# Rotating 96 images by 90 degrees: loads moved from the SyncE queue to the GpSimd queue, the last slab first

## The chip, the cores and the metric

The kernel runs on one core of a Trainium2 chip. A core has compute engines (TensorE or PE, VectorE or DVE, ScalarE or ACT, GpSimd or POOL) and a queue engine, SyncE or SP, that only issues transfers and waits. Transfers between the chip's main memory (HBM) and the on-chip memory (SBUF, 128 partitions) are carried out by 16 DMA engines, whoever issues them. The metric is the device time of one execution in microseconds (us); lower is better. The times given for the kernel before are 123.1, 123.25 and 123.28 us: a median of 123.25 us.

## The reference

```python
def setup_inputs():
    batch, c, h, w = 32, 3, 256, 256
    return {"x": np.random.randn(batch, c, h, w).astype(np.float32)}

def reference(x):
    return np.rot90(x, k=-1, axes=(-2, -1)).astype(np.float32)
```

There are 32 x 3 = 96 images of 256 x 256 float32 values. Each is turned clockwise by a quarter: the output's row c is the input's column c read from the bottom row upwards. Nothing is computed; 25.17 MB are read, rearranged and 25.17 MB are written.

## The kernel before, in words

**Slabs.** The 96 images are cut into 12 slabs, 0 to 11, of 8 images or 2 MB each (`n_slabs` = 12, `last` = 11). A slab lies in SBUF as one buffer of 128 partitions x 4096 values, and is called `units[n]`. Two layouts are in use. In the short one a partition holds pieces of 8 image rows (8 KB in one run), and in the long one a transfer of 1 MB fills every second partition with 16 image rows (16 KB in one run). Slabs 0, 1 and 2 are loaded short and stored long; the others are loaded long. All 12 slabs stay resident, so no load has to wait for a buffer.

**Loads.** All loads are issued by SyncE, in the order 0, 1, 2, 3, 7, 4, 5, 6, 8, 9, 10, 11 (line 86). Slabs 1 and 2 are one transfer of 2 MB each (line 88); every other slab is two transfers of 1 MB, one for each `i` (lines 92 and 96). The first transfer of slab 11 is cut once more, into 14/16 and 2/16 of its bytes, and the first of these two is remembered as `mark`. The framework gives SyncE's transfers eight completion semaphores in turn, so a ninth transfer waits until the first has landed, and so on.

**Turning.** VectorE turns a slab with transposes of 32 x 32 blocks (line 118), two instructions for a slab or four for a pair of slabs; each handles 128 x 2048 values. The rest of the turn lies in the access patterns. The result of slab n goes to `home[n]`, which is the buffer of slab n-1 (already used up); that of slab 0 goes to PSUM (`turned0`). Slabs 8 and 9 are turned as a pair into the buffers of slabs 3 and 7, and slabs 10 and 11 as a pair into the buffers of slabs 8 and 9. So the pair 8/9 can't be turned before slab 4's result, which stands in the buffer of slab 3, is stored.

**Stores.** All stores are issued by SyncE too, behind the loads in its queue, in the order 4, 3, 5, 6, 7, 1, 2, 8, 9, 10, 11, 0: 17 transfers of 1 or 2 MB (lines 124, 127, 130 and 132). The store of slab 4 waits for `mark`, so that stores begin when nearly all loads have landed (line 139). The result of slab 0 is copied by ScalarE from PSUM into the buffer of slab 11 (line 146) once VectorE has read that buffer, and it is stored last.

**Order on the queues.** SyncE works through its instructions in program order: an instruction that waits holds up all that follow. GpSimd does nothing in this kernel apart from four small fills of constants that the framework puts at its start.

Of the kernel before, what the change touches and what calls it, by code (L numbers as in the profile page):

```python
# [1 line left out]

# [4 lines left out]

@with_exitstack
def kernel(
    ctx: ExitStack,
    tc: tile.TileContext,
    x: bass.AP,
    out: bass.AP,
):

    nc = tc.nc
    fp32 = mybir.dt.float32

    B, C, H, W = x.shape
    P = nc.NUM_PARTITIONS
    RL, RS = 16, 8  # L50
    I = 2
    Q = P * RS // H
    n_slabs = B * C // (Q * I)
    last = n_slabs - 1
    F = RS * W
    long_st = (0, 1, 2)
    both = (8, 10)
    paired = [n + a for n in both for a in range(2)]

    rows_in = x.rearrange("b c h w -> (b c h) w")  # L60
    rows_out = out.rearrange("b c h w -> (b c h) w")

    def short(rows):
        return rows.rearrange("(n i p r) w -> n p i (r w)", i=I, p=P, r=RS)

    def long(rows):
        return rows.rearrange("(n i m r) w -> n i m (r w)", i=I, m=P // I, r=RL)

    ld_short, ld_long, st_short, st_long = short(rows_in), long(rows_in), short(rows_out), long(rows_out)

    units = [None] * n_slabs
    adjacent = [(3, 7), (8, 9), (10, 11)]
    pairs = []
    for us in adjacent + [(u,) for u in range(n_slabs) if all(u not in us for us in adjacent)]:
        pool = ctx.enter_context(tc.tile_pool(name=f"unit{us[0]}", bufs=1))
        held = pool.tile([P, len(us), I * F], fp32, name=f"u{us[0]}")
        for j, u in enumerate(us):
            units[u] = held[:, j]
        pairs.append(held)
    psum = ctx.enter_context(tc.tile_pool(name="psum", bufs=1, space=bass.MemoryType.PSUM))  # L80
    turned0 = psum.tile([P, I * F], fp32, name="turned0")

    def fours(t):
        return t.rearrange("p (i f) -> p i f", i=I)

    for n in (0, 1, 2, 3, 7, 4, 5, 6, *range(8, n_slabs)):
        if n in (1, 2):
            nc.sync.dma_start(out=fours(units[n]), in_=ld_short[n])
            continue
        for i in range(I):  # L90
            if n in long_st:
                ld = nc.sync.dma_start(out=fours(units[n])[:, i], in_=ld_short[n][:, i])  # L92
            else:
                cuts = (0, 14 * W, RL * W) if (n, i) == (last, 0) else (0, RL * W)
                for f0, f1 in zip(cuts, cuts[1:]):
                    ld = nc.sync.dma_start(out=units[n][i::I, f0:f1], in_=ld_long[n, i][:, f0:f1])
                    if f1 == 14 * W:
                        mark = ld

    home = [turned0] + units[:last]  # L100

    def turn(n):
        if n in long_st:
            src = fours(units[n]).rearrange("p i (r g c) -> p c r g i", r=RS, c=RL)
            dst = home[n].rearrange("p (c k r) -> p c r k", c=RL, r=RS)[:, :, ::-1, ::-1]
            parts, step = 2, RL // 2
        elif n in paired:
            if n not in both:
                return
            src = pairs[both.index(n) + 1].rearrange("p a (r g c) -> p c r g a", r=RL, c=RL)  # L110
            dst = pairs[both.index(n)].rearrange("p i (c k r) -> p c r k i", c=RL, r=RL)[:, :, ::-1, ::-1, :]
            parts, step = 4, RL // 4
        else:
            src = units[n].rearrange("p (r g c) -> p c r g", r=RL, c=RS)
            dst = fours(home[n]).rearrange("p i (c k r) -> p c r k i", c=RS, r=RL)[:, :, ::-1, ::-1, :]
            parts, step = 2, RS // 2
        for h in range(parts):
            nc.vector.transpose(out=dst[:, h * step : (h + 1) * step], in_=src[:, h * step : (h + 1) * step])  # L118

    def store(n):  # L120
        if n in paired:
            first = n if n in both else n - 1
            if n == first:
                nc.sync.dma_start(out=st_long[n].transpose([1, 0, 2]), in_=pairs[both.index(n)][::I])
                return
            for i in range(I):
                nc.sync.dma_start(out=st_long[n, i], in_=pairs[both.index(first)][n - first :: I, i])
        elif n in long_st:
            for i in range(I):
                nc.sync.dma_start(out=st_long[n, i], in_=home[n][i::I])  # L130
        else:
            return nc.sync.dma_start(out=st_short[n], in_=fours(home[n]))

    for n in range(both[0]):
        turn(n)
    for n in (4, 3, 5, 6, 7, 1, 2):
        st = store(n)
        if n == 4:
            tc.add_manual_dep(st.ins, mark.ins.name, mybir.DependencyInfo(
                mybir.DependencyClass.Sync, mybir.DependencyReason.SCHED_ONLY), reason="stores after loads")  # L140
    for n in range(both[0], n_slabs):
        turn(n)
        store(n)

    for i in range(I):
        nc.scalar.copy(out=fours(units[last])[:, i], in_=fours(turned0)[:, i])  # L146
    home[0] = units[last]
    store(0)


# [1 line left out]
_INS = ['x']  # L152
_OUTS = [((32, 3, 256, 256), 'float32')]


# [23 lines left out]
```

## Time and profile before

| | value |
|---|---|
| times of three runs | 123.1, 123.25, 123.28 us |
| profiled execution: span from first to last instruction | 121.4 us |
| difference of median and span | 1.8 us |
| bytes moved, DMA queue 1 (issued by SyncE) | 50.33 MB in 4800 packets, 98.0% of 16 engines' span |
| VectorE busy | 90.5 us (75%), 24 instructions |
| ScalarE busy | 4.9 us |
| GpSimd busy | 0.2 us |

The profile is of one execution. A packet is the unit in which a DMA engine's work is recorded: here one contiguous run of 8 or 16 KB (14 and 2 KB for the cut transfer), or the 4 bytes by which an engine reports that its share of a transfer is done. "SPq" is SyncE's instruction queue and "DVEq" VectorE's. A group of instructions is given as line, engine, operation and the names of what is written and read; "L118" is line 118. The table of windows cuts the span into stretches and gives for each the engines' busy time, the mean busy share of the 16 DMA engines (a little over 1 where packets overlap) and the bytes moved per time. A DMA transfer "lands" when its completion semaphore has its full count.

### The profile page before, as it was taken

Reading aid. Unit: us, or ns where it says so; the run is one execution under the profiler, and the core shown is the slowest. Engines: PE = TensorE matmul, PEld = TensorE weight load, DVE = VectorE, ACT = ScalarE, POOL = GpSimd, SP = SyncE. Lnnn points to the kernel's source line nnn. Section 1 sums busy time; section 2 is a strip of 40 time slices with the busy share of each in tenths; the row PEclk is TensorE's granted clock in tenths of the full one; section 3 lists DMA queues with packets and bytes.
Section 4 is the critical chain, followed back from the end, with each engine's and each line's share of the span. In section 5 each row is a group of like instructions: output and inputs, shape, how many; then the busy total and the mean of one; then the engine's idle time right before and its main releaser. Section 6 shows DMA issues by size and latency. Waiting matters only on the chain.

```text
span 121.4 us, 134 instructions
## 1 busy us (share of the span) xinstructions
DVE 90.5 (75%) x24; ACT 4.9 (4%) x3; POOL 0.2 (0%) x4
## 2 busy tenths in 40 slices
DVE  0029999999999999999999999999999960000000
ACT  0000000000000000000040000000000038000000
POOL 0000000000000000000000000000000000000000
DMA  3999999999999999999999999999999999999994
GB/s 84 416 432 424 426 459 432 432 432 426 426 432 426 416 421 432 421 426 450 403 424 426 426 429 429 421 432 424 464 426 432 432 432 432 432 432 432 432 432 178
DMA packets 4800, 50.33 MB, mean 414 GB/s; under 512 B 640, under 2 KB 640, under 8 KB 704
## 3 DMA queue, kind: packets, MB, share of 16 engines
q1 hardware_dynamic: 4800, 50.33, 98.0%
HBM read 25.17 MB, written 25.17 MB: 414 GB/s over the span
## 4 chain that ended last, share of the span: by engine, by line
DVE 55%; issue 17%; DMA 6%; DVEq 3%; ACT 2%; ACTq 1%; SPq 0%
DVE u L118 50%; DVE turned L118 6%; DMA u<-in_x_dram 6%; DVEq L174 3%; ACT u L146 2%; ACTq L174 1%; SPq L92 0%; DVEq L118 0%
## 5 line engine op out<-in xcount | busy, mean ns | idle before, releaser
L118 DVE STREAM_TRANSPOSE u<-u 128x2048 f32<-128x2048 f32 x22 | 83.4, 3861 | 0.3
L118 DVE STREAM_TRANSPOSE turned<-u 128x2048 f32<-128x2048 f32 x2 | 7.1, 3584 | 8.3 <-DMA u<-in_x_dram 8.3
L146 ACT COPY u<-turned 128x2048 f32<-128x2048 f32 x2 | 3.6, 1869 | 35.6 <-DVE u L118 35.6
L146 ACT ACT_TABLE_LOAD x1 | 1.3, 1283 | 62.3 <-DMA u<-in_x_dram 62.3
L163 POOL MEMSET const-uint8-127<- 128x1 uint8 x1 | 0.1, 103 | 0.0
L163 POOL MEMSET const-bfloat16-1.0<- 128x1 bf16 x1 | 0.1, 101 | 0.0
L163 POOL MEMSET const-float32-0.0<- 128x1 f32 x1 | 0.1, 99 | 0.2 <-issue 0.2
L163 POOL MEMSET const-float32-1.0<- 128x1 f32 x1 | 0.1, 99 | 0.0
## 6 DMA issues: line engine op xcount, KB each, us to landing
u<-in_x_dram SPq DMA_DIRECT2D x19, 1024.0 KB, 19.6
out_dram<-u SPq DMA_DIRECT2D x7, 2048.0 KB, 16.3
out_dram<-u SPq DMA_DIRECT2D x10, 1024.0 KB, 18.3
u<-in_x_dram SPq DMA_DIRECT2D x2, 2048.0 KB, 13.7
u<-in_x_dram SPq DMA_DIRECT2D x1, 896.0 KB, 19.3
u<-in_x_dram SPq DMA_DIRECT2D x1, 128.0 KB, 17.2
```

Source lines behind the costliest of these rows:

```text
L118: nc.vector.transpose(out=dst[:, h * step : (h + 1) * step], in_=src[:, h * step : (h + 1) * step])
L146: nc.scalar.copy(out=fours(units[last])[:, i], in_=fours(turned0)[:, i])
L163: nc = _bacc.Bacc("TRN2", target_bir_lowering=False, num_devices=1)
L174: with _tile.TileContext(nc) as tc:
```

## The change

The order of the loads becomes 11, 0, 1, 2, 3, 7, 4, 5, 6, 8, 9, 10. The two transfers of slab 11 are issued by SyncE. All others, 22 transfers of 1 MB, are issued by GpSimd, in the order given, with the option that the share of each DMA engine in a transfer is one packet (`single_packet=True`). Slabs 1 and 2 are loaded as two transfers each, and slab 11's first transfer is no longer cut. `mark` is now the first transfer of slab 10, the last but one that GpSimd issues. The stores stay on SyncE in their old order, which is now spelled out by ordering hints between one store and the next; the first waits for `mark`. VectorE's and ScalarE's work is the same.

```diff
-    for n in (0, 1, 2, 3, 7, 4, 5, 6, *range(8, n_slabs)):
-        if n in (1, 2):
-            nc.sync.dma_start(out=fours(units[n]), in_=ld_short[n])
-            continue
+    def pull(out, in_):
+        if in_slab == last:
+            return nc.sync.dma_start(out=out, in_=in_)
+        ld = nc.gpsimd.dma_start(out=out, in_=in_, single_packet=True)
+        if behind:
+            tc.add_manual_dep(ld.ins, behind[-1].ins.name, mybir.DependencyInfo(
+                mybir.DependencyClass.NoSync, mybir.DependencyReason.SCHED_ONLY), reason="order of the loads")
+        behind.append(ld)
+
+    behind = []
+    for in_slab in (last, 0, 1, 2, 3, 7, 4, 5, 6, *range(8, last)):
+        n = in_slab
         for i in range(I):
             if n in long_st:
-                ld = nc.sync.dma_start(out=fours(units[n])[:, i], in_=ld_short[n][:, i])
+                pull(out=fours(units[n])[:, i], in_=ld_short[n][:, i])
             else:
-                cuts = (0, 14 * W, RL * W) if (n, i) == (last, 0) else (0, RL * W)
-                for f0, f1 in zip(cuts, cuts[1:]):
-                    ld = nc.sync.dma_start(out=units[n][i::I, f0:f1], in_=ld_long[n, i][:, f0:f1])
-                    if f1 == 14 * W:
-                        mark = ld
+                pull(out=units[n][i::I], in_=ld_long[n, i])
+    mark = behind[-2]
...
+    tail = [mark]
+
+    def put(out, in_):
+        st = nc.sync.dma_start(out=out, in_=in_)
+        tc.add_manual_dep(st.ins, tail[0].ins.name, mybir.DependencyInfo(
+            mybir.DependencyClass.Sync if tail[0] is mark else mybir.DependencyClass.NoSync,
+            mybir.DependencyReason.SCHED_ONLY), reason="order of the stores")
+        tail[0] = st
...
     for n in (4, 3, 5, 6, 7, 1, 2):
-        st = store(n)
-        if n == 4:
-            tc.add_manual_dep(st.ins, mark.ins.name, mybir.DependencyInfo(
-                mybir.DependencyClass.Sync, mybir.DependencyReason.SCHED_ONLY), reason="stores after loads")
+        store(n)
```

In `store`, each `nc.sync.dma_start` becomes `put` with the same operands.

## The prediction

> **What bounds the kernel now.** I read the page first, from its top.
>
> ```profile
> span 121.4 us, 134 instructions
> DVE 90.5 (75%) x24; ACT 4.9 (4%) x3; POOL 0.2 (0%) x4
> DMA  3999999999999999999999999999999999999994
> q1 hardware_dynamic: 4800, 50.33, 98.0%
> ```
>
> VectorE is busy for three quarters of the span, the DMA engines in every slice but the first and the last. The chain of waits puts 55% on VectorE, but that chain ends in stores, and what holds them is the row of DMA. So I read the bytes per time by stage, in a table of windows (columns: stretch, its length, DVE, ACT and POOL busy, clock, DMA share, GB/s).
>
> ```profile
> 2.00:3.00 1.00, 0.00 (x0) 0.00 (x0) 0.00 (x0) 1.00 0.44 164
> 3.00:16.00 13.00, 7.71 (x3) 0.00 (x0) 0.00 (x0) 1.00 1.01 425
> 19.00:57.00 38.00, 37.83 (x11) 0.00 (x0) 0.00 (x0) 1.00 1.01 428
> 62.50:78.00 15.50, 15.47 (x5) 1.05 (x1) 0.00 (x0) 1.00 1.01 427
> 108.00:119.00 11.00, 0.00 (x0) 0.00 (x0) 0.00 (x0) 1.00 1.00 429
> ```
>
> Loads of 8 KB packets run at 425 GB/s and of 16 KB at 428; stores of 8 KB at 427 and of 16 KB at 429. There is no hole from 3 to 119 us, the turn from loads to stores included. The time is therefore a start, 50.33 MB at this rate, and an end; a change counts only if it alters the rate or opens a hole. For holes I read SyncE's waits and the timeline.
>
> ```profile
> SPq L96 <- DMA u<-in_x_dram: 32.5, 14, 4.5
> SPq L174 <- DMA out_dram<-u: 15.0, 5, 5.5
> SPq L132 <- DMA u<-in_x_dram: 13.9, 1, 13.9
> ```
>
> ```profile
> 0.73 0.88 SPq L92 DMA_DIRECT2D u<-in_x_dram  x2
> 8.25 7.08 DVE L118 STREAM_TRANSPOSE turned<-u 128x2048 f32<-128x2048 f32 x2 [8.25 <-DMA u<-in_x_dram]
> 15.36 83.70 DVE L118 STREAM_TRANSPOSE u<-u 128x2048 f32<-128x2048 f32 x22
> 59.46 11.13 SPq L132 DMA_DIRECT2D out_dram<-u  x5
> 99.10 0.63 SPq L124 DMA_DIRECT2D out_dram<-u  x1
> 102.76 2.67 SPq L130 DMA_DIRECT2D out_dram<-u  x2
> ```
>
> Fourteen loads wait for an earlier landing, and the first store waits 13.9 us for `mark`; neither empties the DMA engines. VectorE, once started, never stops until 99.1 us. The last store is issued some 16 us ahead of the end. In the packet records the first data starts at 1.77 us and the last ends at 120.3.
>
> **The sum's base.** The profiled span is 121.43 us, the median 123.25. The 1.82 us between them lie outside the profile, and I leave them as they are.
>
> **Part 1: rate of the 22 moved loads.** One engine's share of 1 MB is 64 KB: 8 packets in slabs 0 to 2, 4 in the others. At 425 GB/s an engine needs 8192 / (425/16) = 308.4 ns for 8 KB; at 428, 612.5 ns for 16 KB. Two small packets take 4.3 ns more than a large one, so a packet costs about 4.3 ns beside its bytes (3 to 6 with the rounding of the rates). With one packet for 64 KB, six transfers save 7 x 4.3 ns and sixteen save 3 x 4.3 ns: 0.18 + 0.21 = 0.39 us. All of it is on the path, since the DMA engines have no other idle time. No row shows a load issued by GpSimd, so this is bounded. Best: the 23.07 MB, which take 6.29/0.425 + 16.78/0.428 = 54.0 us, run at the best rate that the packet costs allow for stores (429 without 4.3 ns in 611 ns is 432 GB/s), 53.4 us, and 22 completion packets of 9 ns vanish as well: 0.8 us saved. Worst: the nearest row of a queue that is not fed by SyncE is the instruction queue, whose six 8 KB packets took 475 ns against 309 in the load queue. If each transfer lost these 166 ns once, uncovered, it would be +3.7 us. I take the saving of 0.39: the instruction packets ran one at a time before the span on an idle memory, while here up to eight transfers stand in line, and the first packets of SyncE's own loads (0.7 to 1.3 us) show that a cold packet says little about the stream.
>
> The Trainium skill ("DMA: Bandwidth & Descriptors", section "Why small descriptors are slow (HBM only)") gives about 3 cycles of overhead a packet and calls joining descriptors worthwhile only at 256 B or less; by its fabric clock of 850 MHz that is an estimated 3.5 ns, near the row's 4.3, and the sum would be 0.32 us. The same page ("Latency and other measured facts") speaks against the change: engines 7 and 15 are usually slower under GpSimd's descriptor rings; it gives no figure, and no row here can show it.
>
> **Part 2: the start.** SyncE issues slab 11 at the same 0.73 us, two issues as now, so data starts at the same 1.77 us. Its 2.1 MB keep the engines busy for 4.9 us, to 6.7. GpSimd's fills end at 0.43; its issue is not shown. The nearest rows are SyncE's, from 0.47 (load) to 1.4 us (store in pieces), and from issue to first data SyncE takes 1.04, so GpSimd's first data should come by 2.9 us. It costs nothing up to 6.7, and the excess one for one after that. The ramp could differ by 0.3 us either way (six of sixteen engines started 0.7 us late; slab 11 has half as many packets). Taken: 0.
>
> **Part 3: VectorE starts later.** Slab 0 now shares the engines with slab 11: between +0 and +4.9 us, if all of slab 11 goes first. What covers it is the queue of stores. After VectorE ends (99.1) the stores of slabs 10, 11 and 0 follow, 6.3 MB or 14.7 us; data ends near 120.0, so the engines run dry at 105.3 and the store must be issued by 104.2. That is 5.1 us of cover for at most 4.9. Slab 0's store needs the copies and issues behind it (3.6 + 1.3 + 1.0 = 5.9 us), covered by 9.8 us of slabs 10 and 11. Pair 8/9 needs slab 4 stored, which landed at 67.1 against 70.5. Price 0; past 5.1 us it is one for one. Later slabs come every 4.9 us and are used every 7.6, so they are never late.
>
> **Part 4: queues.** GpSimd issues 22 loads, of which 14 wait for the eighth before them, as 14 do on SyncE now. With seven or eight 1 MB transfers in line (17 us) an issue may take up to 2.44 us, the time of 1 MB, before it limits anything. Nothing else stands in that queue. SyncE's 17 stores stand behind the wait for `mark`, as they stood behind the loads.
>
> **Part 5: loads to stores.** `mark` landed at 59.39, 0.47 us behind its last data; the store was issued at 59.46, and its first packet ran at 61.26, when the loads ran out. With 1.04 us from issue to data it was ready at 60.5, some 0.76 us early. Now 1 MB follows `mark` in place of 1.125 MB: 0.3 us less, 0.45 early. Cost 0, unless a GpSimd landing reports over 0.45 us later than a SyncE one.
>
> **Part 6: the end.** SyncE waits for every completion semaphore; there are up to eight more, in pairs of 0.065 us (event at 120.64, next at 120.70). Between 0, if they stand ahead of the last store's, and 0.26. I take one, 0.06: the early ones are paired with late ones today.
>
> **Sum.** -0.39 + 0.06 = -0.33 us: a span of 121.1 and a time of 122.92 us, 0.27% less.
>
> **Rivals.**
>
> *The ring-fed queue is slower (other side).* Place: the 54 us of the moved loads. If each transfer, or one of the 16 engines, loses more than it saves, the loads stretch and everything behind them moves. It decides from (0.33 + 0.25) / 22 = 26 ns a transfer, a load rate under about 425 GB/s. At half the 166 ns it is +1.8 us less the saving: 124.7; in full 126.6. For it: the 475 ns row. Against: eight transfers in line. Where it decides I put it at 124.2, a mild loss of 60 ns a transfer (+1.3 us) less the rest.
>
> *The option or queue changes no rate.* The DMA share is already 1.01 and packets overlap, so the 4.3 ns may belong to runs of bytes rather than to packets. Then parts 2 to 6 alone are left: 123.3.
>
> *GpSimd and VectorE stand in each other's way.* Transposes run back to back (3861 ns each, 0.3 us idle in all). If GpSimd could prepare a transfer only between two of them, one transfer in 3.9 us would replace one in 2.44: 14 x 1.4 = +20 us, about 143. No row shows GpSimd working beside a transpose.
>
> The Trainium skill ("SBUF — State Buffer", section "SBUF: two separate sides") warns of just this for VectorE's two-port modes; a transpose at 2048 values in 3.86 us is 0.53 a ns, under one per cycle of the 0.96 GHz that it states, so by the rule it should not bite: 0 instead of 20 us.
>
> *A hole at the turn or the start.* A landing 0.45 + x late, or first GpSimd data at 6.7 + x, costs x: 123.5 to 124.5.
>
> **How the numbers follow.** Less than 0.2%, about 0.25 us, cannot be told from no change. Forecast with its mechanism: 0.48, of which 0.40 falls beyond 0.2% (its own range 122.2 to 123.1). No rate change: 0.12. Slower queue: 0.28. Engines in each other's way: 0.04. Hole: 0.08. Faster: 0.40 and 0.02 from luck at the start, 0.42. Same: 0.08 and 0.10: 0.18. Slower: 0.40. The low end, 122.2, is 123.25 less 0.8 and the 0.3 of the ramp; the high end takes in the slower queue up to half of its upper bound and a bit, 125.2. Outside stay the far part of the slower queue (0.10), the collision (0.04) and a little below.
>
> **What would show it.** Right: load stretches at 430 GB/s or more, loads over by 60.5 to 61 us, no dip in the first five slices or at the turn, VectorE starting between 9 and 13 us and ending by 104, fewer packets. Wrong: a load stretch under 425 GB/s, a slice under 9 before the stores, waits of VectorE on loads after its start, or longer transposes. The forecast falls if engines drift apart in the loads, which the mean rate hides but the turn would show.

## The result

The changed kernel takes 123.96 us (median of 4 runs, 123.83 to 124.05) against 123.2 us before (123.1 to 123.28): the ratio is 1.0062 with a 95% interval of 1.0048 to 1.0077. It is slower by 0.76 us, or 0.6%. The forecast was 122.92, faster.

### The profile page after: what moved, and what is told of

The parts are those of the page before. It is cut to its first block, busy times and chain, and to the rows that moved or that the text cites. A ratio compares the mean times of both kernels' runs of the same rounds, so it can differ in the third digit from the quotient of the medians.

```text
span 122.2 us, 145 instructions
## 1 busy us (share of the span) xinstructions
DVE 90.5 (74%) x24; ACT 4.9 (4%) x3; POOL 11.9 (10%) x26
## 3 DMA queue, kind: packets, MB, share of 16 engines
q0 software_dynamic: 2144, 23.07, 44.5%
## 4 chain that ended last, share of the span: by engine, by line
DVE 41%; DMA 25%; issue 15%; DVEq 3%; ACT 2%; ACTq 1%; POOL 1%; PEldq 0%
DVE u L123 41%; DMA u<-in_x_dram 25%; DVEq L185 3%; ACT u L157 2%; ACTq L185 1%; POOL u L89 1%; DVEq L123 0%; PEldq L185 0%
## 5 line engine op out<-in xcount | busy, mean ns | idle before, releaser
L123 DVE STREAM_TRANSPOSE turned<-u 128x2048 f32<-128x2048 f32 x2 | 7.1, 3586 | 13.4 <-DMA u<-in_x_dram 13.4
L89 POOL DMA_DIRECT2D u<-in_x_dram x22 | 11.7, 534 | 31.5 <-DMA u<-in_x_dram 30.7
## 6 DMA issues: line engine op xcount, KB each, us to landing
out_dram<-u SPq DMA_DIRECT2D x10, 1024.0 KB, 13.5
```

Source lines behind the costliest of these rows:

```text
L89: ld = nc.gpsimd.dma_start(out=out, in_=in_, single_packet=True)
```

## The profile after

The page of the changed kernel, its lines on busy time, slices, DMA queues and VectorE's first work:

```profile
span 122.2 us, 145 instructions
DVE 90.5 (74%) x24; ACT 4.9 (4%) x3; POOL 11.9 (10%) x26
DMA  3999999999999999999999999999999999999993
...
q1 hardware_dynamic: 2608, 27.26, 53.0%
q0 software_dynamic: 2144, 23.07, 44.5%
...
L123 DVE STREAM_TRANSPOSE turned<-u 128x2048 f32<-128x2048 f32 x2 | 7.1, 3586 | 13.4 <-DMA u<-in_x_dram 13.4
```

The span grew from 121.4 to 122.2 us. The row of DMA still has no slice under 9 between the first and the last. GpSimd's 23.07 MB are a queue of their own (q0). Its 2144 packets are 768 of 8 KB, 1024 of 16 KB and 352 completions: one data packet for each run of bytes. Nothing was merged into packets of 64 KB.

The table of windows of the changed kernel (stretch, length, busy times, clock, DMA share, GB/s):

```profile
3.00:16.00 13.00, 2.59 (x1) 1.28 (x1) 3.59 (x7) 1.00 0.98 413
19.00:57.00 38.00, 37.83 (x11) 0.00 (x0) 5.35 (x11) 1.00 1.01 431
62.50:78.00 15.50, 15.43 (x5) 0.00 (x0) 0.00 (x0) 1.00 1.01 429
108.00:119.00 11.00, 0.00 (x0) 0.00 (x0) 0.00 (x0) 1.00 1.01 429
```

This view books whole packets, so a few GB/s either way mean nothing. If each packet record is spread over its own time, the loads from 24 to 57 us run at 428.4 GB/s in both kernels, and a load packet takes the same median time from GpSimd's queue after as from SyncE's before, 613 ns for 16 KB and 309 ns for 8 KB. The first line, 413 against 425 before, holds the later start: spread in the same way, the loads from 4 to 16 us run at 425.8 GB/s against 426.2. The stream is as fast as it was, and no faster.

The timeline of the changed kernel:

```profile
0.73 1.20 SPq L88 DMA_DIRECT2D u<-in_x_dram  x2
1.23 4.31 POOL L89 DMA_DIRECT2D u<-in_x_dram  x8 [0.79 <-PEq L185]
...
13.41 7.08 DVE L123 STREAM_TRANSPOSE turned<-u 128x2048 f32<-128x2048 f32 x2 [13.41 <-DMA u<-in_x_dram]
...
20.52 83.67 DVE L123 STREAM_TRANSPOSE u<-u 128x2048 f32<-128x2048 f32 x22
...
60.01 49.76 SPq L128 DMA_DIRECT2D out_dram<-u  x17
104.22 3.63 ACT L157 COPY u<-turned 128x2048 f32<-128x2048 f32 x2 [92.62 <-DVE u L123]
```

SyncE's first two loads took 1.20 us to issue; the two it issued first before took 0.88. VectorE starts at 13.4 in place of 8.25 and ends at 104.2 in place of 99.1.

So where are the 0.76 us? The packet records and landings of the two profiled executions cut each span into three parts:

```
                          before    after    difference
first data                  1.77     2.10      +0.33
first to last data        118.50   118.54      +0.04
last data to last landing   0.35     0.35       0.00
last landing to end         0.81     1.19      +0.38
span                      121.43   122.18      +0.75
```

The 118.5 us in which data move are as long as before, to 0.04 us. The start and the end became longer.

What SyncE does in the end can be seen in the instructions of the framework's closing line (minimum/median/maximum ns, first and last start). Before:

```profile
L174 SPq EVENT_SEMAPHORE  x7: 17/28/28, 110.9 to 121.4; - x7
L174 POOLq EVENT_SEMAPHORE_RANGE_CLEAR  x1: 93/93/93, 121.1 to 121.1; - x1
```

After:

```profile
L185 SPq EVENT_SEMAPHORE  x11: 17/28/28, 109.8 to 122.1; - x11
L185 POOLq EVENT_SEMAPHORE_RANGE_CLEAR  x1: 136/136/136, 121.8 to 121.8; - x1
```

There are four more waits, and clearing takes 43 ns more. What counts is their order. Each instruction waits for two semaphores; the times are their starts, after the last data:

```
before: last landing 120.62 on semaphore 107
  120.637 waits for 107 and 102;  120.702 the drain that follows
after: last landing 120.99 on semaphore 110
  121.005 waits for 110 and 103
  121.066 111, 102;  121.126 112, 101;  121.187 113, 100
  121.246 114, 99;   121.308 116, 109;  121.373 the drain that follows
```

All of the later five pairs had been satisfied long before, the latest DMA landing among them at 113.7 us. They still cost 0.061 us each, one after the other, because they stand behind the last store's semaphore.

## The experiments

My theory after the result was: the start costs 0.33 us because SyncE's first load now has the long form (every second partition, 16 KB each); the end costs 0.38; the option and GpSimd's queue cost and gain nothing. The rivals were that GpSimd's queue, or the option, slows the loads in itself, and that only the order matters. For the time of each comparison the kernel before ran beside it, at 123.24 to 123.29 us.

**Without the option.**

```diff
-        ld = nc.gpsimd.dma_start(out=out, in_=in_, single_packet=True)
+        ld = nc.gpsimd.dma_start(out=out, in_=in_)
```

> The changed kernel without the single-packet option on GpSimd's loads. Theory (start + end): the option does nothing that can be seen, since the changed kernel's own records show 8 and 16 KB packets and between 6 and 9 us the two queues share at 2:1, the ratio of one 16 KB piece to one 8 KB piece; so 123.9 to 124.0 us, first data at 2.1, the same 2:1 sharing, loads at 428 GB/s. Rival (the option costs or saves time): loads differ from 428 by more than 2 GB/s, the sharing changes, and the time moves by over 0.3 us.

Measured: 124.01 us, ratio 1.006 (1.0047 to 1.0073), first data at 2.10 us, 428.4 GB/s. Its page:

```profile
DMA packets 4752, 50.33 MB, mean 412 GB/s; under 512 B 656, under 2 KB 656, under 8 KB 656
...
q0 software_dynamic: 2144, 23.07, 44.5%
```

The number of packets is the same as with the option. From 6 to 9 us, where both queues have work, the packet records give these rates (SyncE's packets are 16 KB in the first two kernels and 8 KB in the third, GpSimd's are 8 KB):

```
GB/s, 6 to 9 us                GpSimd   SyncE
changed kernel                   134      296
without the option               149      282
SyncE loads slab 0 (next run)    214      215
```

The engines alternate run by run, 1 to 2 where the runs are 8 and 16 KB and 1 to 1 where they are equal. That agrees with the Trainium skill ("DMA: Bandwidth & Descriptors", section "Queues, rings and completion order"), which has each engine change between queues after each packet, if a packet here is one run; the 9 to 17 descriptors a packet that the section calls typical don't fit these shares, where a descriptor is one run. Had GpSimd's packet been 64 KB beside SyncE's single runs of 16 KB, it would have been 4 to 1 for GpSimd. In this kernel the option does nothing that a record or a time shows.

**Slab 0 in place of slab 11 as SyncE's load.**

```diff
-        if in_slab == last:
+        if in_slab == 0:
-    for in_slab in (last, 0, 1, 2, 3, 7, 4, 5, 6, *range(8, last)):
+    for in_slab in (0, 1, 2, 3, 7, 4, 5, 6, *range(8, n_slabs)):
```

> The changed kernel with slab 0 in place of slab 11 as the one that SyncE loads first; slab 11 goes last on GpSimd's queue. Theory (start + end): first data returns to 1.77 us and VectorE starts near 8.3, while the end keeps its 1.54 us behind the last data: 123.5 to 123.65 us, a ratio to the kernel before of 1.003. Rival (GpSimd's queue itself slows the loads): 123.9 or more, as in the changed kernel. Rival (only slab 11 going first costs): 123.2.

Measured: 123.68 us, ratio 1.0034 (1.0022 to 1.0046). First data at 1.78 us, last landing to end 1.18. VectorE started only at 10.7, since GpSimd's slabs share the engines with slab 0's second half. The start is back and the end is not. The stretch of data was 0.19 us longer than in the kernel before: from 88 to 118 us the stores ran at 428.3 GB/s, against 430.9 before and 430.4 in the changed kernel, and no run shows why. The timeline:

```profile
0.74 0.87 SPq L88 DMA_DIRECT2D u<-in_x_dram  x2
1.24 4.31 POOL L89 DMA_DIRECT2D u<-in_x_dram  x8 [0.79 <-PEq L185]
```

**The order of the loads alone, GpSimd unused.**

```diff
-    for n in (0, 1, 2, 3, 7, 4, 5, 6, *range(8, n_slabs)):
+    for n in (last, 0, 1, 2, 3, 7, 4, 5, 6, *range(8, last)):
...
-                cuts = (0, 14 * W, RL * W) if (n, i) == (last, 0) else (0, RL * W)
-                for f0, f1 in zip(cuts, cuts[1:]):
-                    ld = nc.sync.dma_start(out=units[n][i::I, f0:f1], in_=ld_long[n, i][:, f0:f1])
-                    if f1 == 14 * W:
-                        mark = ld
+                ld = nc.sync.dma_start(out=units[n][i::I], in_=ld_long[n, i])
+                if (n, i) == (last - 1, 0):
+                    mark = ld
```

> The kernel before with its order of loads alone changed: slab 11 first and in two uncut transfers, the mark on slab 10's first transfer, all loads still issued by SyncE. Theory (start + end): first data at 2.1 us, the end as before (1.16 us): 123.45 to 123.65 us, with VectorE starting near 13.1 and no hole in the stores. Rival (GpSimd's queue is the whole cause): 123.2.

Measured: 123.68 us, ratio 1.0036 (1.0024 to 1.0048), with first data at 2.09 us:

```profile
0.72 1.21 SPq L94 DMA_DIRECT2D u<-in_x_dram  x2
1.98 1.25 SPq L92 DMA_DIRECT2D u<-in_x_dram  x2
```

The slow first issue belongs to the load of slab 11 and not to GpSimd, which issues nothing here. As the first on SyncE's queue, an issue of slab 11 takes 0.57 to 0.58 us and its first data come 0.79 us after, in every kernel that begins with it; one of slab 0 takes 0.39 to 0.41, and data come 0.64 after. Whether it's the larger runs, the stepping over every second partition or the place of slab 11 in memory was not tested apart, since no other long load went first. Nor does the form alone set the length of an issue: behind slab 11, the two of slab 0 took 0.59 and 0.62 us here. VectorE started at 13.5 and ended at 104.4, and the row of DMA has no hole. The end was 0.88 and not 0.81: 39 transfers in place of 40 left one pair behind the last landing. I had expected no change there, and this was the hint for what follows.

**Eight small transfers on GpSimd, added to the kernel before.** They add semaphores only, and nobody reads what they load.

```diff
+    few = ctx.enter_context(tc.tile_pool(name="few", bufs=1))
+    for k in range(8):
+        bit = few.tile([1, 64], fp32, name=f"bit{k}")
+        nc.gpsimd.dma_start(out=bit, in_=rows_in[k : k + 1, :64])
```

> The kernel before plus eight transfers of 256 bytes issued by GpSimd at the start, which nobody uses: they add eight completion semaphores and next to no data. Theory (start + end): SyncE waits at the end for five more pairs of semaphores, 0.061 us each, and their clearing takes 0.04 more: the end behind the last data grows from 1.16 to 1.5 us, the time to 123.5 to 123.7 us. Rival (the end is longer because 23 MB went through GpSimd's queue): the end stays at 1.16 us and the time at 123.2 to 123.3.

Measured: 123.87 us, ratio 1.0047 (1.0034 to 1.0061), and the expectation was wrong in its mechanism. There are as many waits as in the changed kernel:

```profile
L178 SPq EVENT_SEMAPHORE  x11: 17/28/28, 105.7 to 121.9; - x11
```

But the last landing was at 121.11 and the end 0.88 us later, so only 0.07 was added. The time went elsewhere: the stretch of data grew to 119.0 us. It had 413 GB/s between 5 and 10 us, where the small packets run, against 425 before (0.14 us), 428.1 from 88 to 118 us against 430.9 (0.2 us), and one engine ending 0.17 us after the rest. Why the late stores ran slower is not shown. The number of semaphores alone doesn't set the end. The place of the last store's semaphore does: here 115 was the last of SyncE's eight, as 107 is before. SyncE uses eight in turn; 40 transfers end on the eighth, 19 on the third.

**All loads on GpSimd.**

```diff
-        if in_slab == last:
-            return nc.sync.dma_start(out=out, in_=in_)
-    for in_slab in (last, 0, 1, 2, 3, 7, 4, 5, 6, *range(8, last)):
+    for in_slab in (0, 1, 2, 3, 7, 4, 5, 6, *range(8, n_slabs)):
```

> The changed kernel with all 24 loads on GpSimd, in the old order, nothing loaded by SyncE. In the changed kernel GpSimd's first packet ran at 5.2 us, 3.9 us after its first issue began at 1.23. Reading A (GpSimd's first transfer takes that long by itself): first data near 5.2 us, so 3.4 us later than before, and with a longer end about 127 us. Reading B (it was only held behind SyncE's packets, which were in the engines first): first data between 2.3 and 3.0 us, about 124.3 to 124.9 us. In both the loads run at 428 GB/s, and the end is about 1.6 us, since the last of 17 SyncE transfers uses the first of its eight semaphores.

Measured: 124.79 us, ratio 1.0129 (1.0106 to 1.0152). Reading B: first data at 2.63 us, 1.40 after the first issue began, with the end at 1.32 us behind the last landing (17 transfers end on the first of the eight semaphores). So GpSimd's first packets, which ran only at 5.0 to 5.4 us in each kernel that has SyncE loads in front, had been held back. Each time SyncE's first 1 MB was about through. Why the engines did not alternate before that isn't settled; they were busy meanwhile, so it cost nothing.

**Slabs 11 and 10 first.** This moves VectorE's start further.

```diff
-        if in_slab == last:
+        if in_slab in (last, last - 1):
-    for in_slab in (last, 0, 1, 2, 3, 7, 4, 5, 6, *range(8, last)):
+    for in_slab in (last, last - 1, 0, 1, 2, 3, 7, 4, 5, 6, 8, 9):
```

> The changed kernel with slabs 11 and 10 both loaded first by SyncE. This tests the cover of VectorE's late start, which the prediction put at an end of VectorE's work by 104.2 us. Theory: slab 0 is complete near 17.5 us, VectorE ends near 108.3, the DMA engines stand empty for 3 to 4 us before the store of slab 10, and the time is 127 to 128 us. Rival (late starts of VectorE are covered further than that): 124 us.

Measured: 128.63 us, ratio 1.0436 (1.0422 to 1.045), somewhat above the expected 127 to 128, since slab 0 was complete at 18.4 and not 17.5. Timeline and windows:

```profile
18.38 7.08 DVE L123 STREAM_TRANSPOSE turned<-u 128x2048 f32<-128x2048 f32 x2 [18.38 <-DMA u<-in_x_dram]
25.49 83.68 DVE L123 STREAM_TRANSPOSE u<-u 128x2048 f32<-128x2048 f32 x22
109.20 3.63 ACT L157 COPY u<-turned 128x2048 f32<-128x2048 f32 x2 [97.55 <-DVE u L123]
```

```profile
100.00:106.00 6.00, 6.00 (x3) 0.00 (x0) 0.00 (x0) 1.00 0.93 393
106.00:110.40 4.40, 3.17 (x1) 1.20 (x1) 0.00 (x0) 1.00 0.00 0
110.40:120.00 9.60, 0.00 (x0) 2.43 (x2) 0.00 (x0) 1.00 1.03 437
```

All 16 engines stand empty from 106.09 to 110.48 us, 4.39 us, until the store of slab 10 starts. VectorE ended 4.98 us later than in the changed kernel, so that kernel had 4.98 - 4.39 = 0.59 us of cover left.

**The changed kernel with 24 transfers on SyncE.**

```diff
-            put(out=st_short[n], in_=fours(home[n]))
+            for i in range(I):
+                put(out=st_short[n][:, i], in_=fours(home[n])[:, i])
```

> The changed kernel with the stores of slabs 3 to 7 cut into two transfers of 1 MB each, so that SyncE issues 24 transfers and not 19. SyncE's eight semaphores are used in turn and waited for at the end in the order of their numbers, so with 24 the last store has the last of them. Theory (the end is set by where the last store's semaphore stands): no pair is left to wait for after the last landing, the end behind the last data falls from 1.54 to 1.2 to 1.25 us and the time from 123.96 to 123.6 to 123.7. Rival (the mere number of semaphores sets it): end and time as in the changed kernel, 1.54 and 123.95.

Measured: 123.79 us, ratio 1.0042 (1.0029 to 1.0054). The semaphores are as many as in the changed kernel, and the part after the last landing fell from 1.19 to 0.88 us, as the theory has it. Four kernels differ here in the number of SyncE's transfers, beside eight semaphores of GpSimd, and their ends line up: 0.88 us with 24, the last on the eighth semaphore of SyncE; 1.06 with 21, on the fifth (two slabs first); 1.19 with 19, on the third; 1.32 with 17, on the first. That is 0.06 us a place. The time fell by 0.17 us, or by 0.25 if each kernel is taken against the kernel before that ran beside it. That is less than 0.31: in the profiled execution, the slowest of five, the stretch of data was 0.23 us longer, one engine ending 0.12 us after the others. Whether the cut stores do that, or it varies from run to run, this run alone can't tell; in the last but one run below the same cut stores had 118.47.

**The kernel before with 43 transfers.**

```diff
+            if n in (5, 6, 7):
+                for i in range(I):
+                    nc.sync.dma_start(out=st_short[n][:, i], in_=fours(home[n])[:, i])
+                return
```

> The kernel before with the stores of slabs 5, 6 and 7 cut into two transfers of 1 MB each: 43 transfers on SyncE in place of 40, nothing on GpSimd. Theory (where the last store's semaphore stands): it now has the third of eight, five pairs or so are waited for behind it, the end grows from 1.16 to about 1.45 us and the time from 123.2 to about 123.5. Rival (GpSimd's queue or its semaphores are needed for a longer end): 1.16 us and 123.2.

Measured: 123.39 us, ratio 1.0008 (0.9997 to 1.0019): too close to 1 to call it slower. Three pairs and not five came behind the last landing. With SyncE's eight semaphores alone, the third is waited for together with the fifth, and SyncE stood at that pair until the landing, with three pairs left; so the number of semaphores matters too, through the pairing. The end was 0.98 us in place of 0.81. The direction is as expected, the size is smaller, and only the profile shows it.

**Both terms undone, GpSimd's queue kept.** The edits of the second run and of the one with 24 transfers together.

> The changed kernel with both edits together: SyncE loads slab 0 first, and the stores of slabs 3 to 7 are cut in two, so that SyncE issues 24 transfers. 23.07 MB still go through GpSimd's queue. Theory (start + end, and no cost of GpSimd's queue): first data at 1.77 us, 1.22 us behind the last data, 123.3 to 123.5 us, within 0.2% of the kernel before. Rival (GpSimd's queue costs something of its own, which the two terms hid): 123.6 us or more, from a longer stretch of data or a load rate under 427 GB/s.

Measured: 123.37 us, ratio 1.0008 (0.9999 to 1.0017). Its page and windows:

```profile
span 121.6 us, 150 instructions
...
DMA  3999999999999999999999999999999999999994
```

```profile
19.00:57.00 38.00, 37.83 (x11) 0.00 (x0) 5.24 (x10) 1.00 1.01 429
```

First data at 1.77 us, 118.47 us of data, an end of 0.89 us behind the last landing; that landing came 0.47 us behind the last data, where the kernel before has 0.35, so that the two together are 1.36 and not the expected 1.22. This closes the account to within about 0.1 us: with start and end put right, 23.07 MB through GpSimd's queue cost no more than the measurement can tell, and gain nothing.

**Two issuers for slab 0**, on the kernel before, in search of a better start.

```diff
-                ld = nc.sync.dma_start(out=fours(units[n])[:, i], in_=ld_short[n][:, i])
+                ld = (nc.scalar if i else nc.sync).dma_start(out=fours(units[n])[:, i], in_=ld_short[n][:, i])
```

> The kernel before with the second transfer of slab 0 issued by ScalarE at the same time as SyncE issues the first. In the kernel before eight to ten engines take their first packet at 1.8 us and the others only at 2.5 to 2.7. If the late ones wait for more work to be issued, they start near 1.9 us, and the time falls by 0.1 to 0.3 us to 122.9 to 123.1. If not (they wait for memory, or share one unit that hands out work), the start is as before and the time 123.2 to 123.3.

Measured: 123.42 us, ratio 1.0018 (1.001 to 1.0027). ScalarE issued at the same 0.72 us as SyncE, but its packets began at 2.74 against 1.74, and the start didn't improve: from 3 to 4 us 343 GB/s were moved against 420 before, a loss of 0.18 us. In the profiled execution, the slowest of eleven, the stretch of data was 119.02 us. No version here beats the kernel before.

## Why the prediction was wrong

**Part 1, the saving of 0.39 us by larger packets: 0.** This is the first failed step. Without it the forecast is +0.06 us and no longer a gain; what made the kernel slower are parts 2 and 6. The step took the option at its word, and priced a 64 KB packet. The page after has one packet for each run of bytes, and the run without the option has the same packets, sharing and time. That a 16 KB packet costs some 5 ns less than two of 8 KB (613 against 2 x 309) still holds; the packets just stayed as they were. This was the second rival, "changes no rate". It was right on the rate and, at 123.3, missed what came of the other parts.

**Part 2, the start at 0: +0.33 us.** The step said that SyncE issues two loads "as now". It does not: it issues loads of another form, and as the first of the queue their issue and first data take 0.17 and 0.15 us longer. The trace of the kernel before had a hint, in its loads of slab 0 (L92) and of the long form (L96; minimum/median/maximum ns):

```profile
L96 SPq DMA_DIRECT2D u<-in_x_dram x19: 471/472/601, 3.1 to 45.0; - x19
L92 SPq DMA_DIRECT2D u<-in_x_dram x2: 407/412/417, 0.7 to 1.2; - x2
```

The bound of 0.3 us either way came close in size by luck: it stood for the ramp of the engines and for half as many packets, not for a slower issue.

**Part 6, the end at 0.06 with a bound of 0.26: +0.38 us.** This term was mis-sized. I counted more semaphores; what counts is how many pairs stand behind the last store's, and with GpSimd's eight semaphores beside SyncE's that follows from the number of SyncE's transfers, 19 in place of 40. Five pairs at 0.061, 0.04 for clearing and 0.03 around it make the 0.38.

**Sum.** 0.39 + 0.33 + 0.32 make 1.04 of the 1.08 us between the forecast change of -0.33 and the +0.75 in the span; the last 0.04 is the stretch of data.

**The signs.** The four signs of being wrong that I named watch the stream, and what failed were the ends. None of them came, but for the 413 GB/s from 3 to 16 us, which is the later start. Two signs of being right seem to be there and mean nothing. The table of windows has 431 GB/s for the loads, by its booking of whole packets, and there are 48 fewer packets, because the uncut load of slab 11 has 64 fewer and one transfer more has 16 completions.

**Part 3, VectorE's late start at 0: right, by luck and by little.** All of slab 0 came behind most of slab 11: VectorE started 5.2 us later, past the 4.9 that I had as the worst and the 5.1 that I had as the cover, and ended exactly at the 104.2 that I gave as the limit. The limit was 0.6 us too strict, as the two slabs first show. Nearly half of that is in my sum, which took the end of the data at 120.0 us where the packet records have 120.3.

**Parts 4 and 5: right.** GpSimd needed 0.53 us an issue, against a limit of 2.44. At the turn to stores the engines stayed full, at least 15.9 of 16 packets in work on average in every quarter of a microsecond; the rate dipped to some 385 GB/s for a microsecond, which is 0.1 us, where the kernel before has a smaller dip at its cut transfer.

**The other rivals.** A slower queue: refuted, the load rate is 428.4 in both, and the last run but one puts an upper end of 0.17% on all that is left. The warning of the Trainium skill on engines 7 and 15 ("DMA: Bandwidth & Descriptors", section "Latency and other measured facts") shows in no rate here; the records don't tell the engines apart, but all together they are as fast from either queue. GpSimd and VectorE in each other's way: refuted. The six transposes into SBUF that ran beside an issue of GpSimd take 3975 ns on average, the same six of the kernel before 3978. GpSimd's first issue takes 0.66 us and the others 0.52 to 0.53, before the transposes and during them, as the rule in "SBUF — State Buffer" (section "SBUF: two separate sides") let one expect. A hole: none.

## What to carry to other kernels

Here the DMA engines were full from the first data to the last, moving transfers to another queue left the rate as it was, and so only the two ends could change, by tenths of a microsecond. In such a case read the issue of the very first load, by its form, and what the issuing queue does after the last landing. Before an option is priced, look for a row that would show it at work; without one, "it does nothing" deserves more than 0.12. And where completion semaphores are used in turn and waited for in order, as here, count the transfers: the end was shortest where the last one landed on the last semaphore.

## What I had not expected of the hardware

Which load is issued first moves the start by 0.3 us, and the one with fewer and larger runs is the slower (0.57 us to issue against 0.41). GpSimd's packets did not begin until 5.0 to 5.4 us while SyncE's first 1 MB was in the engines, though alone they begin 1.40 us after the issue; ScalarE's queue, at 2.74, was not held back like that. And a wait that is satisfied already takes SyncE 0.061 us at the end of the program.
